# Logits of two heads issued in alternation, and large tiles placed at multiples of 1024 bytes

## Chip, cores and metric

The kernel runs on one core of one Trainium2 chip. The metric is device time in microseconds (us) of one execution; the kernel before is given as the median of three runs.

## What is computed

One layer of a decoder trunk on 256 tokens of width 2048, all in float32. From the reference, cut to what the text below uses:

```python
proj = x @ w_in[l] + b_in[l]
q, k, v, zb, uc, gl = jnp.split(proj, offs, axis=-1)
# A: dilated window attention, 24 heads of 64 (three groups of 8)
logits = jnp.einsum('brnqhd,brnkhd->brnhqk', qb, kb)
logits = jnp.where(mask, logits * (hd ** -0.5) + bias, NEG_INF)
p = jnp.exp(logits - m); den = jnp.sum(p, axis=-1, keepdims=True)
o = jnp.einsum('brnhqk,brnkhd->brnqhd', p, vb) / den
# the three groups' outputs are weighted by their denominators and summed
yb = _spatial_gating(jax.nn.gelu(zb), ...)                # B
yc = jax.nn.gelu(_s5(uc, ...)); yc = yc * sigmoid(yc @ w_glu[l] + b_glu[l])   # C
merged = gates_a * (ya @ w_pa[l]) + gates_b * (yb @ w_pb[l]) + gates_c * (yc @ w_pc[l])
x = _layer_norm(ALPHA * x + merged @ w_o[l], ln1_g[l], ln1_b[l])
gate_f, up = jnp.split(x @ w_ffn_in[l], 2, axis=-1)
x = _layer_norm(ALPHA * x + (silu(gate_f) * up) @ w_ffn_out[l], ln2_g[l], ln2_b[l])
```

## The kernel before

All large products use TensorE's fp32r type with operands split in two: a value is hi + lo, and hi*hi + hi*lo + lo*hi is summed in PSUM. A **unit** is one 512 KB block of weights (eight 128x128 blocks, or two of 128x512). For each unit SP issues a load into a `raw` tile, ScalarE copies it to `wh` (`split_h`, L262), VectorE subtracts to get `wl` (`split_l`, L268), and TensorE runs the unit's matmuls. There are four buffers of each of the three.

Two forms of unit carry the time. In a *wide* unit the activations move and the weights stand: for each of eight k-blocks a 512-column matmul (L79, hi weights against hi and lo of `xT` or `x1T`, which lie side by side) and a 256-column one (L80, lo weights). It is used for q, k, zu, uc, the gates, the GLU and the first FFN product. In a *tall* unit the weights move and 128 columns of the activations stand: three matmuls of 512 columns (L165, L166, L167; 384 columns for zv) per k-block and half of the tokens. It is used for v (`xT` stands), zv (`xT`), the output projection (`m`) and the second FFN product (`h0` for the first 12 of 44 k-blocks, and tiles `h1`... of the pool `s6` for the other 32).

The main loop over units calls `step_tasks(True)` once per unit, after the unit's matmuls are issued: it advances the generator `attention()` by one step, to its next `yield`. All engines take their instructions in this written order, SP's loads too. `attention()` is started after v; its steps fall into the 12 zu units and the 16 zv units, and are used up there.

For a pair of heads `hp` (0 to 3) and its half `e` (rows 0-63 or 64-127 of `q` and `k`), attention does: logits of the three groups for two blocks of 128 tokens, 6 matmuls in full float32 into two PSUM banks (L691, L694; each is run as two passes); softmax on VectorE and ScalarE (L699 to L706); 8 transposes and two copies (L712, L716). Each is one step, so there are three steps to a head. `values(hp)` (L662) multiplies with v for both heads of a pair, at the start of the step that issues the next pair's first logits. `load_bias` (L643) fetches a head's table of position bias for one block by four DMAs of 64 KB; two blocks are fetched one head ahead, at the step of the logits.

Tiles of SBUF come from pools in the order of first use. In the built program the pool `const` begins at byte 16512 of each partition; each tile is rounded up to 32 bytes (`bcol` 384, `ident` 512, `eps` 8, `s5keep` 576), so the large tiles begin at byte 18016, which is 608 past a multiple of 1024. `xT`/`x1T`, `x_raw`/`z0`/`z`, `raw`, `wh`, `wl` and `h0` follow without gaps in sizes that are multiples of 1024, so all of them lie at 608 past a multiple. Then comes `s5i` (96 bytes), and the eleven `s6` tiles behind it (`q`, `k`, `v`, `m`, `yb`, `yc`, `h1`..., 6144 bytes each) lie at 704 past a multiple. A 128-column block of fp32r has 512 bytes, so a block within a tile begins at 96 past a multiple of 512 in the first set, and at 192 in `s6`.

Of the kernel before, what the change touches and what calls it, by code (L numbers as in the profile page):

```python
# [10 lines left out]
F32 = mybir.dt.float32  # L11
F32R = mybir.dt.float32r
I32 = mybir.dt.int32
AF = mybir.ActivationFunctionType
ALU = mybir.AluOpType
# [10 lines left out]
NJ = 24  # L26
# [6 lines left out]
def hybrid_layer(ctx: ExitStack, tc: tile.TileContext, d: dict, out: bass.AP):  # L33
    nc = tc.nc
    const = ctx.enter_context(tc.tile_pool(name="const", bufs=1))
    sb = ctx.enter_context(tc.tile_pool(name="sb", bufs=1))
    psp = ctx.enter_context(tc.tile_pool(name="psp", bufs=1, space=bass.MemoryType.PSUM))
    dram = ctx.enter_context(tc.tile_pool(name="dram", bufs=1, space=bass.MemoryType.DRAM))
    V, A, G, T = nc.vector, nc.scalar, nc.gpsimd, nc.tensor

    RAW_BUFS, HL_BUFS, AHEAD = 4, 4, 4

    def bank(tag="mm"):
        return psp.tile([128, 512], F32, tag=tag, bufs=4, name=f"ps_{tag}")

    def tmp(n=512):

        if n <= 256:
            t = sb.tile([128, 256], F32, tag="t1", bufs=6, name="tmp1")
        else:  # L50
            t = sb.tile([128, 512], F32, tag="t2", bufs=6, name="tmp2")
        return t[:, :n]

    def s6(shape, dt, name):
        return sb.tile(shape, dt, tag="s6", bufs=11, name=name)

    def copy_split(hi, lo, src, scale=1.0):
        A.activation(hi, src, AF.Copy, scale=scale)  # L58
        if scale == 1.0:
            V.tensor_tensor(lo, src, hi.bitcast(F32), op=ALU.subtract)  # L60
        else:
            V.scalar_tensor_tensor(lo, src, scale, hi.bitcast(F32), op0=ALU.mult, op1=ALU.subtract)
# [177 lines left out]
    with tc.manual_schedule():  # L240
# [60 lines left out]
        s5 = {}  # L301
        bcol = const.tile([128, 96], F32, name="bcol")
        ident = const.tile([128, 128], F32, name="ident")


        def actx(k):
# [14 lines left out]
        big = {}  # L321
# [24 lines left out]
        def post_v(g):  # L346
            def post(ps):
                bv = big["row"]
                for t in range(2):
                    if g == 0:  # L350
                        big["v", t] = s6([128, 1536], F32, f"v{t}")
                    V.tensor_tensor(big["v", t][:, g * 512:(g + 1) * 512], ps[t], bv, op=ALU.add)
                if g == 2:
                    marks["att"] = spawn(attention(), first=True)
            return post
# [22 lines left out]

        def s5_setup():
            P = s5["P"]  # L380
            PI = sb.tile([128, NJ], I32, tag="s5i", bufs=1, name="s5i")
            keep = const.tile([128, 3, NJ, 2], F32, name="s5keep")
            bm = s6([128, 2, NJ, 32], F32, "bm")
            bb = s6([128, 2, NJ, 32], F32, "bb")
# [6 lines left out]
            def new():  # L391
                return P[:, free.pop(), :]

            pt = new()

            def ts(o, a, s1, s2, op0, op1=None):
                if op1 is None:
                    G.tensor_scalar(o, a, s1, None, op0=op0)
                else:
                    G.tensor_scalar(o, a, s1, s2, op0=op0, op1=op1)  # L400

            def tt(o, a, b, op):
                G.tensor_tensor(o, a, b, op=op)
# [7 lines left out]
            def exp(x):  # L411
# [7 lines left out]
                for c in (1.0 / 120, 1.0 / 24, 1.0 / 6, 0.5, 1.0, 1.0):  # L419
                    tt(p, p, r, ALU.mult)  # L420
                    ts(p, p, c, None, ALU.add)
                ts(PI, k, 126.0, 8388608.0, ALU.add, ALU.mult)
                tt(p, p, PI.bitcast(F32), ALU.mult)
                ts(p, p, 2.0, None, ALU.mult)
# [3 lines left out]
            th, k, r, q, x = new(), new(), new(), new(), new()  # L428
# [10 lines left out]
            n2, t, cr, ci = new(), new(), new(), new()  # L439
# [6 lines left out]
            s, c = new(), new()  # L446
# [43 lines left out]
            for c3 in range(3):  # L490
                ps = bank("sd")
                for c2 in range(2):
                    for ri in range(2):
                        c = c3 * 2 + c2
# [148 lines left out]
        def load_bias(h, t):  # L643
            bt = tmp()
            a = big["tab"][h]
            for rr in range(2):
                rq = 2 * t + rr
                for half, blk in ((0, 3 - rq), (1, 7 + 2 * (1 - rr))):
                    src = bass.AP(tensor=a.tensor, offset=a.offset + blk * 127 + 63,
                                  ap=[[L_TAB - 1, 64], [127, 4], [1, 64]])  # L650
                    nc.sync.dma_start(bt[rr * 64:(rr + 1) * 64, half * 256:half * 256 + 256]
                                      .rearrange("p (a b) -> p a b", a=4), src)
            return bt

        def attention():
            order = [(hp, e) for hp in range(4) for e in range(2)]
            big["ya"] = [s6([128, 2, 512], F32R, f"ya{i}") for i in range(2)]
            nxt = [load_bias(0, t) for t in range(2)]
            yield
            pT = [[big["z0"][:, 12 + 2 * t:14 + 2 * t, :].rearrange("p a b -> p (a b)") for t in range(2)], None]  # L660

            def values(hp):  # L662
                ya = bank("sd")
                for t in range(2):
                    for c in range(4):
                        g = max(0, c - 1)
                        vt = c if c < 2 else t
                        for e in range(2):
                            vc = (8 * g + 2 * hp + e) * 64
                            T.matmul(ya[64 * e:64 * e + 64, t * 128:(t + 1) * 128], lhsT=big["v", vt][:, vc:vc + 64],  # L670
                                     rhs=pT[e][t][:, c * 128:(c + 1) * 128], start=c == 0, stop=c == 3,
                                     tile_position=(0, 64 * e))
                y = big["ya"][hp // 2][:, hp % 2, :]
                copy_split(y[:, 0:256], y[:, 256:512], ya[:, 0:256])

            for n, (hp, e) in enumerate(order):
                if n and e == 0:
                    values(hp - 1)
                pr = slice(64 * e, 64 * e + 64)
                p = nxt  # L680
                if n + 1 < 8:
                    hp1, e1 = order[n + 1]
                    nxt = [load_bias(2 * hp1 + e1, t) for t in range(2)]
                lg = [bank("sd"), bank("sd")]
                for t in range(2):
                    for g in range(3):
                        f = 4 * g + hp
                        qa = big["q", f // 6][pr, f % 6, t * 128:(t + 1) * 128]
                        ka = big["k", f // 6][pr, f % 6, :]
                        if g == 0:  # L690
                            T.matmul(lg[t][:, 0:256], lhsT=qa, rhs=ka, start=True, stop=True)  # L691
                        else:
                            o = lg[t][:, 256:512].rearrange("p (a g i) -> p a g i", a=2, g=2)[:, :, g - 1, :]
                            T.matmul(o, lhsT=qa, rhs=ka[:, t * 128:(t + 1) * 128], start=True, stop=True)  # L694
                yield
                pn = [tmp(256), tmp(256)]
                sm = [sb.tile([128, 4], F32, tag="sm", bufs=4, name="sm") for _ in range(2)]
                for t in range(2):
                    V.tensor_tensor_reduce(p[t], lg[t], p[t], -1.0, 3.0e38, ALU.add, ALU.min, sm[t][:, 0:1])  # L699
                    A.activation(p[t], p[t], AF.Exp, bias=sm[t][:, 0:1], scale=-1.0, accum_out=sm[t][:, 1:2])  # L700
                for t in range(2):
                    V.reciprocal(sm[t][:, 2:3], sm[t][:, 1:2])
                    V.tensor_scalar(pn[t].rearrange("p (g a i) -> p a g i", a=2, g=2),
                                    p[t][:, 256:512].rearrange("p (a g i) -> p a g i", a=2, g=2),
                                    sm[t][:, 2:3], None, op0=ALU.mult)
                    V.tensor_scalar(p[t][:, 0:256], p[t][:, 0:256], sm[t][:, 2:3], None, op0=ALU.mult)  # L706
                yield
                pt = [bank("sd"), bank("sd")]
                for t in range(2):
                    for c in range(4):  # L710
                        src = (p[t] if c < 2 else pn[t])[:, (c % 2) * 128:(c % 2 + 1) * 128]
                        T.transpose(pt[t][:, c * 128:(c + 1) * 128], src, ident)  # L712
                if e == 1:
                    pT[1] = [tmp(), tmp()]
                for t in range(2):
                    A.activation(pT[e][t], pt[t], AF.Copy)  # L716
                yield
            values(3)


        def gmlp():
# [485 lines left out]
        while top_up():  # L1207
            pass
        marks["s5"] = spawn(s5_setup())
        for n, u in enumerate(units):  # L1210
            pos["n"] = n
# [138 lines left out]
```

## Time and profile before

| | before |
|---|---|
| median of 3 runs | 1602.92 us (1602.57 to 1603.49) |
| profiled execution, its own time | 1604.32 us |
| its span, first to last instruction | 1602.6 us |
| mean granted TensorE clock | 0.995 |
| TensorE busy | 99% |
| VectorE, ScalarE, GpSimd busy | 58%, 48%, 35% |
| DMA (mean busy share of 16 engines) | 0.6, 192 GB/s |

A matmul's busy time overlaps with the next one's, so rates are read here from starts: the time from the first start of a line to its last, divided by the number of steps between.

### The profile page before, as it was taken

What the parts mean: (1) busy time and instruction counts of PE and PEld (TensorE: products, weight loads), DVE (VectorE), ACT (ScalarE), POOL (GpSimd) and SP (SyncE); (2) the same over time, 40 slices, a digit from 0 to 9 for tenths busy, and PEclk for the clock granted to TensorE, in tenths of its full rate; (3) what the DMA queues carried; (4) which work ended last, traced back from release to release, by engine and by line L of the source; (5) the groups of instructions that cost most, each with busy time, mean ns of one, the idle gap of its engine ahead of it and who ended that gap; (6) DMA issues with size and microseconds to landing.
All of it is one profiled execution on the core that took longest, in us unless ns stands there. A gap on an engine that the chain in (4) does not pass through costs nothing.

```text
span 1602.6 us, 24113 instructions
## 1 busy us (share of the span) xinstructions
PE 1580.8 (99%) x9094; PEld 1366.3 (85%) x9094; DVE 931.0 (58%) x1232; ACT 763.8 (48%) x1040; POOL 559.9 (35%) x1147
## 2 busy tenths in 40 slices
PE   8999999999999999999999999999999999999996
PEld 7888888898999998889789888888888888888885
DVE  5444555556855565469667556565555555445455
ACT  5444434456544444475444545554444544333342
POOL 7569999933999999203011000000000000000002
PEclk9999999999999999999999999999999999999998
DMA  8575557655656555557863565555555556666663
GB/s 275 176 251 186 187 203 207 155 148 188 211 188 198 194 184 194 178 164 209 286 222 118 190 193 184 184 184 184 186 185 192 183 193 237 204 187 192 186 188 101
DMA packets 106492, 307.50 MB, mean 192 GB/s; under 512 B 27567, under 2 KB 28079, under 8 KB 106120
## 3 DMA queue, kind: packets, MB, share of 16 engines
q1 hardware_dynamic: 106280, 305.82, 59.7%
q8 instruction: 71, 1.16, 0.3%
q14 instruction: 45, 0.37, 0.1%
q0 software_dynamic: 96, 0.15, 0.0%
HBM read 303.78 MB, written 5.53 MB: 193 GB/s over the span
## 4 chain that ended last, share of the span: by engine, by line
PE 94%; DVE 3%; DMA 1%; ACT 1%; issue 0%; POOL 0%; SPq 0%; POOLq 0%; ACTq 0%
PE ps_mm L79 40%; PE ps_mm L80 20%; PE ps_mm L165 9%; PE ps_mm L166 9%; PE ps_mm L167 9%; DVE wl L268 1%; PE ps_mm L857 1%; PE ps_mm L858 1%; PE ps_mm L856 1%; PE ps_sd L522 1%; PE ps_sd L691 1%; PE ps_mm L108 0%; PE ps_mm L111 0%; PE ps_sd L670 0%; DMA ln<-in_ln_g_dram 0%
## 5 line engine op out<-in xcount | busy, mean ns | idle before, releaser
L268 DVE TENSOR_TENSOR wl<-raw,wh 128x1024 fp32r<-128x1024 f32 (+1 forms) x544 | 654.2, 1227 | 167.1 <-ACT wh L262 166.6
L262 ACT ACTIVATE wh<-raw 128x1024 fp32r<-128x1024 f32 (+1 forms) x544 | 556.7, 1024 | 369.1 <-PE ps_mm L167 171.6
L79 PE MATMUL ps_mm<-xT,wh 128*128 128x512 f32 x1344 | 480.6, 400 | 6.6 <-ACT wh L58 5.9
L79 PE MATMUL ps_mm<-x1T,wh 128*128 128x512 f32 x1344 | 474.9, 399 | 0.0
L80 PE MATMUL ps_mm<-xT,wl 128*128 128x256 f32 x1344 | 378.9, 282 | 0.5 <-DVE wl L268 0.5
L80 PE MATMUL ps_mm<-x1T,wl 128*128 128x256 f32 x1344 | 377.5, 281 | 0.0
L79 PEld LDWEIGHTS ps_mm<-xT,wh 128*128 128x128 f32 x1344 | 254.3, 189 | 67.1 <-ACT wh L58 5.9
L79 PEld LDWEIGHTS ps_mm<-x1T,wh 128*128 128x128 f32 x1344 | 252.6, 188 | 63.0
L937 POOL TENSOR_TENSOR z<-z,ln2w 128x512 f32<-128x512 f32 (+1 forms) x4 | 5.2, 1302 | 732.5 <-ACT z L936 732.5
L80 PEld LDWEIGHTS ps_mm<-xT,wl 128*128 128x128 f32 x1344 | 256.1, 191 | 1.5 <-DVE wl L268 0.8
L80 PEld LDWEIGHTS ps_mm<-x1T,wl 128*128 128x128 f32 x1344 | 253.9, 189 | 0.0
L546 POOL TENSOR_TENSOR X<-X,t 128x48 f32<-128x48 f32 x255 | 129.1, 506 | 48.6 <-ACT X L526 48.6
L544 POOL TENSOR_TENSOR t<-s5keep,X 128x48 f32<-128x48 f32 x254 | 126.6, 498 | 44.5 <-ACT X L526 24.7
L547 POOL TENSOR_TENSOR X<-X,t 128x48 f32<-128x48 f32 x255 | 129.9, 509 | 20.0
L166 PE MATMUL ps_mm<-wl,h 128*128 128x512 f32 x340 | 134.1, 394 | 0.0
L165 PE MATMUL ps_mm<-wh,h 128*128 128x512 f32 x340 | 134.1, 394 | 0.0
L167 PE MATMUL ps_mm<-wh,h 128*128 128x512 f32 x340 | 134.1, 394 | 0.0
L1037 DVE TENSOR_TENSOR tmp<-ps_mm,tmp 128x256 f32<-128x256 f32 x88 | 37.3, 424 | 152.9 <-ACT tmp L1036 152.9
L545 POOL TENSOR_TENSOR t<-s5keep,X 128x48 f32<-128x48 f32 x254 | 108.5, 427 | 0.0
L315 ACT ACTIVATE tmp<-ps_mm,bcol 128x256 f32<-128x256 f32 x90 | 42.7, 474 | 137.6 <-PE ps_mm L80 137.4
L1036 ACT ACTIVATE tmp<-ps_mm 128x256 f32<-128x256 f32 x88 | 33.8, 384 | 151.6 <-PE ps_mm L80 151.6
L165 PEld LDWEIGHTS ps_mm<-wh,h 128*128 128x128 f32 x340 | 64.0, 188 | 15.0
(214 smaller groups left out, 1775.6 us busy)
## 6 DMA issues: line engine op xcount, KB each, us to landing
raw<-in_w_f_dram SPq DMA_DIRECT2D x264, 512.0 KB, 4.3
raw<-in_w_b_dram SPq DMA_DIRECT2D x164, 512.0 KB, 4.6
raw<-in_w_o_dram SPq DMA_DIRECT2D x32, 512.0 KB, 5.0
raw<-in_w_v_dram SPq DMA_DIRECT2D x24, 512.0 KB, 4.0
raw<-in_w_p_dram SPq DMA_DIRECT2D x32, 384.0 KB, 3.4
raw<-in_w_zv_dram SPq DMA_DIRECT2D x16, 384.0 KB, 3.6
tmp<-tab SPq DMA_DIRECT2D x64, 64.0 KB, 3.2
raw<-in_w_p_dram SPq DMA_DIRECT2D x16, 256.0 KB, 2.9
```

What stands on the lines that cost most here:

```text
L79: T.matmul(ps, lhsT=h[:, j * 128:(j + 1) * 128], rhs=a, start=k == 0, stop=last, skip_group_check=True)
L80: T.matmul(ps[:, 0:256], lhsT=l[:, j * 128:(j + 1) * 128], rhs=a[:, 0:256], start=False, stop=last, skip_group_check=True)
L165: T.matmul(ps[:, :n], lhsT=ah, rhs=hs, start=k == 0, stop=False)
L166: T.matmul(ps[:, :n], lhsT=ah, rhs=ls, start=False, stop=False)
L167: T.matmul(ps[:, :n], lhsT=al, rhs=hs, start=False, stop=k == total - 1)
L262: A.activation(h[:, :m], raws[n][:, :m], AF.Copy)
L268: V.tensor_tensor(l[:, :m], raws.pop(n)[:, :m], h[:, :m].bitcast(F32), op=ALU.subtract)
L315: A.activation(t, ps[:, 256:512], AF.Identity, bias=bcol[:, col:col + 1], scale=scale)
L544: G.tensor_tensor(t1, keep[:, 0], prev, op=ALU.mult)
L545: G.tensor_tensor(t2, keep[:, 1], prev[:, :, ::-1], op=ALU.mult)
L546: G.tensor_tensor(cur, cur, t1, op=ALU.add)
L547: G.tensor_tensor(cur, cur, t2, op=ALU.add)
```

## The change

The eight passes of attention's loop (one per head) become four (one per pair of heads). Within a pass: one step with the 12 logits matmuls of both heads, head 0 and head 1 in turn for each block and group, into four PSUM banks; one softmax step per head; one step of transposes and copies per head, which also issues `load_bias` for the same head of the next pair; one step with `values(hp)`. The number of steps in all is 25 before the last one as before. Four bias tiles are fetched at the first step, where there were two.

Apart from that, `s5i` moves from the pool behind `h0` to `const`, and a tile of 80 floats is put behind it that nothing uses. The `const` pool becomes 96 + 320 bytes longer, so the large tiles begin at byte 18432 = 18 x 1024, and `s6`, with `s5i` gone from in front of it, at 141312 = 138 x 1024. Each tile of both sets, and so each block's offset in 512 bytes, is then 0.

```diff
+    PAD = 80
...
+        s5["i"] = const.tile([128, NJ], I32, name="s5i")
+        const.tile([128, PAD], F32, name="pad")
...
-            PI = sb.tile([128, NJ], I32, tag="s5i", bufs=1, name="s5i")
+            PI = s5["i"]
...
-            nxt = [load_bias(0, t) for t in range(2)]
-            yield
...
-            for n, (hp, e) in enumerate(order):
-                if n and e == 0:
-                    values(hp - 1)
...
-                    nxt = [load_bias(2 * hp1 + e1, t) for t in range(2)]
-                lg = [bank("sd"), bank("sd")]
...
+            p = [[load_bias(e, t) for t in range(2)] for e in range(2)]
+            yield
+            for hp in range(4):
+                lg = [[bank("sd"), bank("sd")] for _ in range(2)]
                 for t in range(2):
                     for g in range(3):
                         f = 4 * g + hp
...
+                        for e in range(2):
+                            pr = slice(64 * e, 64 * e + 64)
+                            qa = big["q", f // 6][pr, f % 6, t * 128:(t + 1) * 128]
+                            ka = big["k", f // 6][pr, f % 6, :]
+                            if g == 0:
+                                T.matmul(lg[e][t][:, 0:256], lhsT=qa, rhs=ka, start=True, stop=True)
+                            else:
+                                o = lg[e][t][:, 256:512].rearrange("p (a g i) -> p a g i", a=2, g=2)[:, :, g - 1, :]
+                                T.matmul(o, lhsT=qa, rhs=ka[:, t * 128:(t + 1) * 128], start=True, stop=True)
+                pn, sm = [None] * 2, [None] * 2
+                for e in range(2):
+                    yield
+                    pn[e] = [tmp(256), tmp(256)]
+                    sm[e] = [soft(p[e][t], lg[e][t]) for t in range(2)]
+                    for t in range(2):
+                        scale(p[e][t], sm[e][t], pn[e][t])
+                for e in range(2):
+                    yield
+                    pt = [bank("sd"), bank("sd")]
...
+                            T.transpose(pt[t][:, c * 128:(c + 1) * 128], src, ident)
...
+                        A.activation(pT[e][t], pt[t], AF.Copy)
+                    if hp < 3:
+                        p[e] = [load_bias(2 * hp + 2 + e, t) for t in range(2)]
+                yield
+                values(hp)
+                yield
```

`soft` and `scale` hold the same VectorE and ScalarE instructions as L699 to L706.

TensorE, at the first logits, before: a step with one head's six matmuls between two wide units.

```order
L80 MATMUL ps_mm<-xT,wl 128x256
L691 MATMUL ps_sd<-k_1794,q_583 128x256
L694 MATMUL ps_sd<-k_1794,q_583 128x2x64
L694 MATMUL ps_sd<-k_2083,q_1505 128x2x64
L691 MATMUL ps_sd<-k_1794,q_583 128x256
L694 MATMUL ps_sd<-k_1794,q_583 128x2x64
L694 MATMUL ps_sd<-k_2083,q_1505 128x2x64
L79 MATMUL ps_mm<-xT,wh 128x512
```

The same place in the changed program (its L80, L81, L702 and L705 are the lines L79, L80, L691 and L694 of before).

```order
L81 MATMUL ps_mm<-xT,wl 128x256
L702 MATMUL ps_sd<-k_1795,q_584 128x256 x2
L705 MATMUL ps_sd<-k_1795,q_584 128x2x64 x2
L705 MATMUL ps_sd<-k_2084,q_1506 128x2x64 x2
L702 MATMUL ps_sd<-k_1795,q_584 128x256 x2
L705 MATMUL ps_sd<-k_1795,q_584 128x2x64 x2
L705 MATMUL ps_sd<-k_2084,q_1506 128x2x64 x2
L80 MATMUL ps_mm<-xT,wh 128x512
```

Each matmul now has its twin of the other head right behind it (x2), on the other 64 rows and into another bank; the second head's step, three units later, is gone.

SP's queue at the start of attention, before (a `tmp` tile is one block's bias, `raw` a unit's weights).

```order
L251 DMA raw<-in_w_b_dram 128x1024 x7
L651 DMA tmp_2805<-tab_680 64x4x64 x4
L651 DMA tmp_2810<-tab_680 64x4x64 x4
L251 DMA raw<-in_w_b_dram 128x1024
L651 DMA tmp_2837<-tab_680 64x4x64 x4
L651 DMA tmp_2842<-tab_680 64x4x64 x4
L251 DMA raw<-in_w_b_dram 128x1024 x3
L651 DMA tmp_2955<-tab_680 64x4x64 x4
L651 DMA tmp_2960<-tab_680 64x4x64 x4
```

And in the changed program.

```order
L252 DMA raw<-in_w_b_dram 128x1024 x7
L654 DMA tmp_2806<-tab_681 64x4x64 x4
L654 DMA tmp_2811<-tab_681 64x4x64 x4
L654 DMA tmp_2816<-tab_681 64x4x64 x4
L654 DMA tmp_2821<-tab_681 64x4x64 x4
L252 DMA raw<-in_w_b_dram 128x1024 x4
L654 DMA tmp_2978<-tab_681 64x4x64 x4
L654 DMA tmp_2983<-tab_681 64x4x64 x4
L252 DMA raw<-in_w_b_dram 128x1024
L654 DMA tmp_3024<-tab_681 64x4x64 x4
L654 DMA tmp_3029<-tab_681 64x4x64 x4
```

Sixteen bias loads now stand ahead of the next weights where eight stood, and later ones come in two consecutive units with one weight load between.

## Rows read from the trace of the kernel before

**Rows 1.** The page's first and fourth part: busy time by engine, last chain by engine.

```profile
PE 1580.8 (99%) x9094; PEld 1366.3 (85%) x9094; DVE 931.0 (58%) x1232; ACT 763.8 (48%) x1040; POOL 559.9 (35%) x1147
...
PE 94%; DVE 3%; DMA 1%; ACT 1%; issue 0%; POOL 0%; SPq 0%; POOLq 0%; ACTq 0%
```

**Rows 2.** The timeline of TensorE at the first logits step: start, duration (both us).

```profile
264.32 0.28 PE L80 MATMUL ps_mm<-xT,wl 128*128 128x256 f32 x1
264.44 0.40 PE L79 MATMUL ps_mm<-xT,wh 128*128 128x512 f32 x1
264.67 0.28 PE L80 MATMUL ps_mm<-xT,wl 128*128 128x256 f32 x1
264.88 0.70 PE L691 MATMUL ps_sd<-k,q 64*128 64x256 f32 x2
265.42 0.60 PE L694 MATMUL ps_sd<-k,q 64*128 64x128 f32 x4
265.86 0.59 PE L691 MATMUL ps_sd<-k,q 64*128 64x256 f32 x2
266.29 0.60 PE L694 MATMUL ps_sd<-k,q 64*128 64x128 f32 x4
266.83 0.50 PE L79 MATMUL ps_mm<-xT,wh 128*128 128x512 f32 x1
```

**Rows 3.** The same view at a step of the state-space branch, which alternates row groups.

```profile
71.40 0.28 PE L80 MATMUL ps_mm<-xT,wl 128*128 128x256 f32 x1
71.61 1.16 PE L522 MATMUL ps_sd<-uT,bbT 32*128 32x128 f32 x16
72.70 0.50 PE L79 MATMUL ps_mm<-xT,wh 128*128 128x512 f32 x1
```

**Rows 4.** Line L165 in v, then in w_ffn_out on `h0`: count, durations (ns), first and last start.

```profile
L165 PE MATMUL ps_mm<-wh,xT x74: 389/389/389, 204.7 to 254.4; 128*128 128x512 f32 x74
...
L165 PE MATMUL ps_mm<-wh,h x17: 389/389/395, 1343.6 to 1354.5; 128*128 128x512 f32 x17
```

**Rows 5.** Line L165 in w_o on `m`, then in w_ffn_out on `s6` tiles.

```profile
L165 PE MATMUL ps_mm<-wh,m x67: 392/397/400, 773.0 to 819.4; 128*128 128x512 f32 x67
...
L165 PE MATMUL ps_mm<-wh,h x49: 389/397/400, 1357.9 to 1391.6; 128*128 128x512 f32 x49
```

**Rows 6.** Line L79 in three stretches of wide units: k, late gates, first FFN product.

```profile
L79 PE MATMUL ps_mm<-xT,wh x227: 395/398/403, 99.8 to 179.7; 128*128 128x512 f32 x114
...
L79 PE MATMUL ps_mm<-xT,wh x117: 391/391/391, 624.8 to 665.0; 128*128 128x512 f32 x117
...
L79 PE MATMUL ps_mm<-x1T,wh x1133: 395/398/403, 899.8 to 1299.8; 128*128 128x512 f32 x189
```

**Rows 7.** Line L856 (merging products, `yc` moves, three 256-column matmuls to a step).

```profile
L856 PE MATMUL ps_mm<-yc,wh x68: 278/280/283, 723.8 to 747.9; 128*128 128x256 f32 x68
```

**Rows 8.** The timeline of VectorE at the second head's softmax, first and last, and behind it.

```profile
277.51 0.69 DVE L699 CUSTOM_DVE_ANT_0 tmp<-ps_sd,tmp 128x512 f32<-128x512 f32 x1
...
280.55 0.42 DVE L706 TENSOR_SCALAR tmp<-tmp,sm 128x256 f32<-128x256 f32 x1
...
282.31 2.52 DVE L268 TENSOR_TENSOR wl<-raw,wh 128x1024 fp32r<-128x1024 f32 x2
```

**Rows 9.** The timeline of TensorE in a zv unit (tall, 384 columns).

```profile
348.25 0.33 PE L166 MATMUL ps_mm<-wl,xT 128*128 128x384 f32 x1
...
348.95 0.34 PE L167 MATMUL ps_mm<-wh,xT 128*128 128x384 f32 x1
```

**Rows 10.** The timeline of SP's queue at the start of attention, then ScalarE's.

```profile
261.59 5.26 SPq L651 DMA_DIRECT2D tmp<-tab  x8
266.96 0.54 SPq L251 DMA_DIRECT2D raw<-in_w_b_dram  x1
267.54 5.19 SPq L651 DMA_DIRECT2D tmp<-tab  x8
...
274.55 1.07 ACT L262 ACTIVATE wh<-raw 128x1024 fp32r<-128x1024 f32 x1
277.36 1.06 ACT L262 ACTIVATE wh<-raw 128x1024 fp32r<-128x1024 f32 x1 [1.74 <-DMA raw<-in_w_b_dram]
```

**Rows 11.** The page's sixth part: one weight load, median us to landing.

```profile
raw<-in_w_b_dram SPq DMA_DIRECT2D x164, 512.0 KB, 4.6
```

More of the change, by code (lines that the diff above doesn't have):

```diff
@@ L655, in attention @@
         def attention():
-            order = [(hp, e) for hp in range(4) for e in range(2)]
             big["ya"] = [s6([128, 2, 512], F32R, f"ya{i}") for i in range(2)]
-            nxt = [load_bias(0, t) for t in range(2)]
-            yield
             pT = [[big["z0"][:, 12 + 2 * t:14 + 2 * t, :].rearrange("p a b -> p (a b)") for t in range(2)], None]
@@ L674, in values, with soft, scale @@
                 copy_split(y[:, 0:256], y[:, 256:512], ya[:, 0:256])
-            for n, (hp, e) in enumerate(order):
-                if n and e == 0:
-                    values(hp - 1)
[L679 to L682, printed above, removed]
-                    nxt = [load_bias(2 * hp1 + e1, t) for t in range(2)]
-                lg = [bank("sd"), bank("sd")]
+            def soft(p, lg):
+                sm = sb.tile([128, 4], F32, tag="sm", bufs=4, name="sm")
+                V.tensor_tensor_reduce(p, lg, p, -1.0, 3.0e38, ALU.add, ALU.min, sm[:, 0:1])
+                A.activation(p, p, AF.Exp, bias=sm[:, 0:1], scale=-1.0, accum_out=sm[:, 1:2])
+                return sm
+            def scale(p, sm, pn):
+                V.reciprocal(sm[:, 2:3], sm[:, 1:2])
+                V.tensor_scalar(pn.rearrange("p (g a i) -> p a g i", a=2, g=2),
+                                p[:, 256:512].rearrange("p (a g i) -> p a g i", a=2, g=2),
+                                sm[:, 2:3], None, op0=ALU.mult)
+                V.tensor_scalar(p[:, 0:256], p[:, 0:256], sm[:, 2:3], None, op0=ALU.mult)
+            p = [[load_bias(e, t) for t in range(2)] for e in range(2)]
+            yield
+            for hp in range(4):
+                lg = [[bank("sd"), bank("sd")] for _ in range(2)]
                 for t in range(2):
@@ L687, in attention @@
                         f = 4 * g + hp
[L688 to L694, printed above, removed]
@@ L695, in attention @@
-                yield
[L696 to L706, printed above, removed]
@@ L707, in attention @@
-                yield
[L708 to L717, printed above, removed]
@@ L718, in attention @@
-            values(3)
+                        for e in range(2):
[7 more added lines that the diff above has]
+                                T.matmul(o, lhsT=qa, rhs=ka[:, t * 128:(t + 1) * 128], start=True, stop=True)
@@ new lines, in attention @@
+                pn, sm = [None] * 2, [None] * 2
[8 more added lines that the diff above has]
+                    pt = [bank("sd"), bank("sd")]
+                    for t in range(2):
+                        for c in range(4):
+                            src = (p[e][t] if c < 2 else pn[e][t])[:, (c % 2) * 128:(c % 2 + 1) * 128]
+                            T.transpose(pt[t][:, c * 128:(c + 1) * 128], src, ident)
+                    if e == 1:
+                        pT[1] = [tmp(), tmp()]
+                    for t in range(2):
+                        A.activation(pT[e][t], pt[t], AF.Copy)
+                    if hp < 3:
+                        p[e] = [load_bias(2 * hp + 2 + e, t) for t in range(2)]
```

## The prediction

> **What bounds the kernel.** I read the page first: TensorE is busy for 99% of the span and makes 94% of the chain that ended last, while no other compute engine passes 58% [rows 1]. So time is won by a shorter stream on TensorE, or lost where that stream is made to wait. Busy time doesn't say how dense the stream is, since matmuls overlap; I therefore took starts. The timeline of TensorE around a step of attention shows what a logits step costs in the stream [rows 2], and the starts of one line over a stretch show the spacing of the large matmuls [rows 4 to 7].
>
> Two things are to be seen there. First, a logits step: from the last L80 ahead of it to the first L79 behind it 266.83 - 264.67 = 2.16 us pass. A wide pair takes (179.7 - 99.8)/226 = 353.5 ns at that time [rows 6]; without the step, the L79 would have followed its L80 by 0.12 us (264.44 - 264.32 in the pair ahead [rows 2]). So a step costs 2.04 us, although it uses only 64 of the 128 rows. Second, equal matmuls don't have equal spacing. A tall 512-column matmul takes (254.4 - 204.7)/73/3 = 227 ns in v and (1354.5 - 1343.6)/16/3 = 227 ns on `h0` [rows 4], but (819.4 - 773.0)/66/3 = 234.3 ns on `m` and (1391.6 - 1357.9)/48/3 = 234.0 ns on the `s6` tiles of h [rows 5]. In rows 4 the moving weights and the standing block both lie 96 bytes past a multiple of 512; in rows 5 the moving operand is at 96 and the standing one at 192. The wide pairs have both at 96, and yet two speeds: 353.5 and (1299.8 - 899.8)/1132 = 353.4 ns in k and in the first FFN product, (665.0 - 624.8)/116 = 346.6 ns in the late gates [rows 6]. The same tiles are used at both speeds, so no address decides that one; it changes only at interruptions of the stream.
>
> **Logits in pairs.** Eight steps of 2.04 us become four. What is one of these worth? The only rows where two row groups alternate are those of the state-space branch: 16 passes of 128 columns take 72.70 - 71.40 = 1.30 us from L80 to L79 [rows 3]. In the logits the two L691 of a block make 0.54 us (264.88 to 265.42) and four passes of 128 columns 0.44 us (265.42 to 265.86), so 0.11 us each, one behind the other [rows 2]. Sixteen of them would take 1.76 us; in rows 3 they took about 0.9, the 1.30 less 0.21 ahead of the first and 0.2 behind the last. So passes on different row groups ran two at a time. Taken over to halves of 64 rows, a step for both heads has the length of one head's step, and 4 x 2.04 = **8.2 us** leave the stream. The other bound is that nothing overlaps: then only the gaps at the borders of a step (0.21 us from L80 to the first pass, and the same from the last of four L694, at 266.29 + 3 x 0.11, to L79) are saved four times, some 0.3 us each less the usual 0.12, 1.2 us in all. I take 8.2, the row being the same kind of instruction with only the size of the group changed.
>
> **What the new order could hold up.** Values, transposes and copies stay as many. Two softmaxes now come in consecutive units. One keeps VectorE for 280.97 - 277.51 = 3.5 us, and a `wl` takes 1.26 (2.52 for two) [rows 8]. Softmax, `wl`, softmax make 8.2 us behind the logits. The second head's transposes are issued four units after them: in zv a unit is 12 x 0.175 = 2.1 us ((348.95 - 348.25)/4 each [rows 9]), so at least 8.4 us and the first head's transposes later, and in zu 11.3. The `wl` in this queue belongs to a unit three further on, so it has 6.3 us or more and needs 4.8. That is covered, with some tenths of a us to spare in zv; if the cover is gone, the loss is bounded by one softmax's excess over a unit, 1.4 us, for each pair, 5 us in all. The four banks for logits: the last to come free is that of `values`, one unit earlier, and its two readers take less than a unit.
>
> SP is moved around too. Eight bias loads take 5.26 us of its queue; sixteen will take 10.5, so that the weights issued at 266.96 go out at about 272.1 [rows 10] and land 4.6 us later [rows 11], at 276.7, where ScalarE wanted them at 274.55. ScalarE splits three units ahead, 8.5 us of wide units, so TensorE doesn't see these 2.1 us. The following weights were issued behind the second eight bias loads before, at 272.7, and are no later now. In later pairs two bursts fall on two consecutive units, 10.5 us of SP for 4.2 to 5.6 us of TensorE, against four `raw` tiles of lead: no more than a us or two per pair where the lead is short. I set 0 and keep up to 3 us in the range, with the 5 above not added, since both would have to come in the same few units.
>
> **Placement.** Everything goes to 0 past a multiple of 512, so the standing block and the moving operand agree in all tall units. If agreement is what separates rows 4 from rows 5, w_o gains 4 x 16 x 2 x 3 = 384 matmuls x (234.3 - 227.0) = 2.8 us, and w_ffn_out, on 32 of its 44 k-blocks, 4 x 32 x 2 x 3 = 768 x (234.0 - 227.0) = 5.4 us: **8.2 us**. v, zv and `h0`, 227 ns and its like now, get nothing. The merging products have 192 against 96 today and take (747.9 - 723.8)/67/3 = 119.9 ns for 256 columns [rows 7], 13.2 above 256 columns at 2.4 GHz, which is what 227 is above 512 columns (13.7): nothing to gain, and a sign that an unequal offset costs only in some patterns. For the wide pairs the offsets agree before and after; their two speeds should go on to depend on how a stretch is entered, and I set 0. The bounds: all pairs at 346.6 would give back 1344 x 6.8 = 9.1 us in the first FFN product and about 576 pairs (uc, q, k, zu) x 6.9 = 4.0 us, together 13.1; the 768 pairs of the gates at 353.4 would cost 5.2.
>
> The Trainium skill ("SBUF — State Buffer", the note on SBUF cachelines) says that SBUF is read at full bandwidth as long as consecutive accesses stay in lines of 16 bytes. All offsets here, 608 and 704, are multiples of 16, so by that rule the placement would change nothing, and the sum would be the pairing's 8.2 alone; the 7 ns between rows 4 and 5 speak for a dependence that the rule doesn't have.
>
> **Sum.** The profiled execution took 1604.3 us, 1.4 above the median. 1604.3 - 8.2 - 8.2 = 1587.9 for it, and 1602.9 - 16.4 = **1586.5 us** for the median.
>
> **Rivals.**
> - *Placement does nothing.* What differs between rows 4 and 5 is then something else, as which unit stands ahead. Against it: within w_ffn_out the same code changes its spacing exactly where the k-blocks leave `h0`. 1602.9 - 8.2 = 1594.7 us.
> - *Wide pairs fall into the faster speed as well.* For it: that speed exists and is kept over 280 us of the gates. Against it: their relative offsets don't change. 1586.5 - 13.1 = 1573.4, or 1577.4 with the first FFN product alone.
> - *The two halves don't overlap.* 1602.9 - 1.2 - 8.2 = 1593.5 us. Rows 3 speak against it.
> - *Multiples of 1024 collide.* With every tile on one phase, standing and moving reads of the wide pairs could meet at L79 and L80 as they do in rows 5. At 7.2 ns for one matmul of each of 2688 pairs, that is 19.4 us: 1605.9; for both, 1625. It turns the sign from 16.4/2688 = 6.1 ns per pair on. Against it: in rows 4 both operands already have one phase in 512 bytes, at the best spacing.
> - *TensorE waits in attention* for softmax or weights, and placement does nothing: 1594.7 + 5 + 3 = 1602.7, no change.
>
> **How the numbers follow.** The forecast, 0.45; faster wide pairs, 0.25; placement without effect, 0.15; no overlap, 0.05; collision, 0.07; waits, 0.03. About 0.2%, 3.2 us, is what a measurement here can tell from no change. The first four are faster by more than that, 0.90; same 0.03; slower 0.07. The range from 1571 to 1596 holds the first four with their bounds of a few us, nine tenths less what lies at their edges.
>
> **What would show it.** Right: each logits step, both heads, still about 2.2 us from L81 to L80 of the new numbering, and four of them; L165's matmuls (L166 in the changed file) at 227 ns on `m` and on all of h; wide pairs at 353 and 347 ns in the stretches where they are now. Wrong: logits steps near 4 us; 234 ns kept in w_o; wide pairs at another spacing than these two, or 347 in the first FFN product; waits of TensorE for `wl`, `tmp` or weights between 262 and 362 us.

## The result and the profile after

| | before | after |
|---|---|---|
| median | 1602.93 us (1602.57 to 1603.49, 4 runs) | 1589.94 us (1588.63 to 1590.49, 4 runs) |
| profiled execution, its span | 1604.32, 1602.6 us | 1590.49, 1588.7 us |
| mean granted TensorE clock | 0.995 | 0.995 |

The ratio is 0.9919 [0.9908, 0.9931]: 13.0 us faster, where 16.4 were forecast; the time lies in the range, 3.4 us above the forecast.

The page of after, its busy times and its last chain, answers to [rows 1]: the bound is the same.

```profile
PE 1566.2 (99%) x9094; PEld 1359.8 (86%) x9094; DVE 931.2 (59%) x1232; ACT 762.9 (48%) x1040; POOL 557.8 (35%) x1147
...
PE 94%; DVE 3%; DMA 1%; ACT 1%; issue 1%; POOL 0%; SPq 0%; POOLq 0%; ACTq 0%
```

With a stream this full, time is told by where the stages start. Each number of this table is the time from the first matmul of a stage to the first of the next (us, profiled runs; w_ffn_out to the start of its last step). The columns on the right are experiments of the next section. Left out are the merging of c (34.6 us, 33.6 in `off32`) and the first four tiles of the first FFN product (about 25 us), which before and after have alike, and what lies ahead of the first matmul and behind the last.

| stage | before | after | pair_only | place_only | not_alternated | off32 | rephase_one |
|---|---|---|---|---|---|---|---|
| uc, q, k | 187.93 | 187.94 | 186.43 | 186.41 | 185.02 | 187.00 | 188.89 |
| v | 65.31 | 65.31 | 65.31 | 65.31 | 65.31 | 67.19 | 65.31 |
| zu | 46.87 | 43.54 | 43.59 | 46.86 | 45.02 | 43.54 | 43.53 |
| zv | 56.61 | 51.90 | 51.90 | 56.63 | 53.37 | 52.00 | 51.89 |
| gates, merging a, b | 329.51 | 332.36 | 329.52 | 332.28 | 332.28 | 331.07 | 331.40 |
| GLU | 23.71 | 24.03 | 23.71 | 24.03 | 24.03 | 23.78 | 24.03 |
| w_o | 93.16 | 90.48 | 91.61 | 90.04 | 89.61 | 92.48 | 90.58 |
| first FFN product | 474.88 | 474.88 | 474.88 | 474.88 | 474.88 | 474.88 | 466.10 |
| w_ffn_out | 244.58 | 238.71 | 244.59 | 238.71 | 238.71 | 243.83 | 238.72 |

From before to after, zu and zv give 3.33 + 4.71 = 8.04 us and w_o and w_ffn_out 2.68 + 5.87 = 8.55; gates and GLU take back 2.85 + 0.32 = 3.17. These make 13.4 of the span's 13.9.

The timeline of TensorE in after at the first logits step (start and duration in us) answers to [rows 2].

```profile
264.30 0.28 PE L81 MATMUL ps_mm<-xT,wl 128*128 128x256 f32 x1
264.50 0.70 PE L702 MATMUL ps_sd<-k,q 64*128 64x256 f32 x4
265.04 0.61 PE L705 MATMUL ps_sd<-k,q 64*128 64x128 f32 x8
265.48 0.60 PE L702 MATMUL ps_sd<-k,q 64*128 64x256 f32 x4
265.92 0.61 PE L705 MATMUL ps_sd<-k,q 64*128 64x128 f32 x8
266.46 0.50 PE L80 MATMUL ps_mm<-xT,wh 128*128 128x512 f32 x1
```

266.46 - 264.30 = 2.16 us, for twice the matmuls: the second head's passes ran wholly beside the first's. The four steps take 2.16, 2.17, 2.22 and 2.22 us, where the eight of before took 2.15 to 2.22.

The next rows are lines of after over a stretch (count, durations in ns, first and last start): L166 on `m` and on the `s6` tiles of h, which answer to [rows 5]; L80 in k, in the late gates and in the first FFN product, which answer to [rows 6]; and a merging product with `yc`, which answers to [rows 7].

```profile
L166 PE MATMUL ps_mm<-wh,m x47: 388/389/390, 774.7 to 806.0; 128*128 128x512 f32 x47
...
L166 PE MATMUL ps_mm<-wh,h x50: 388/390/390, 1345.2 to 1378.6; 128*128 128x512 f32 x50
...
L80 PE MATMUL ps_mm<-xT,wh x227: 394/398/404, 99.8 to 179.7; 128*128 128x512 f32 x114
...
L80 PE MATMUL ps_mm<-xT,wh x114: 394/399/404, 614.8 to 654.7; 128*128 128x512 f32 x114
...
L80 PE MATMUL ps_mm<-x1T,wh x1133: 394/399/404, 889.8 to 1289.8; 128*128 128x512 f32 x189
...
L866 PE MATMUL ps_mm<-yc,wh x96: 282/284/284, 710.6 to 744.8; 128*128 128x256 f32 x96
```

The tall matmuls now follow each other at (806.0 - 774.7)/46/3 = 226.8 and (1378.6 - 1345.2)/49/3 = 227.2 ns in both places, where they took 234. The wide pairs keep 353.5 in k and 353.4 in the first FFN product, but the late gates went from 346.6 to (654.7 - 614.8)/113 = 353.1 ns: a third of the 3.17 us is lost there, most of the rest in the early gates. In these rows and in [rows 6] the durations show it as well, 391 ns for the 512-column matmul of the faster speed and about 398 for that of the slower.

The waits in after from 255 to 365 us (waiting line, releaser: us, times, longest) show whether the new order held up TensorE.

```profile
ACT wh L263 <- DMA raw<-in_w_zv_dram: 10.2, 4, 3.9
...
DVE tmp L679 <- DMA tmp<-tab: 1.3, 2, 1.0
...
PEld ps_sd L702 <- issue: 1.0, 4, 0.3
```

ScalarE waited for weights, up to 3.9 us at a time, and VectorE for a bias. None of TensorE's own waits in this view is longer than 0.3 us; the largest group is the entry into the four logits steps.

### The profile page after: what moved, and what is told of

It reads as the page before. It is cut to its first block, busy times and chain, and to the rows that moved or that the text cites. A ratio compares the mean times of both kernels' runs of the same rounds, so it can differ in the third digit from the quotient of the medians.

```text
span 1588.7 us, 24112 instructions
## 1 busy us (share of the span) xinstructions
PE 1566.2 (99%) x9094; PEld 1359.8 (86%) x9094; DVE 931.2 (59%) x1232; ACT 762.9 (48%) x1040; POOL 557.8 (35%) x1147
## 4 chain that ended last, share of the span: by engine, by line
PE 94%; DVE 3%; DMA 1%; ACT 1%; issue 1%; POOL 0%; SPq 0%; POOLq 0%; ACTq 0%
PE ps_mm L80 40%; PE ps_mm L81 20%; PE ps_mm L166 9%; PE ps_mm L167 9%; PE ps_mm L168 9%; DVE wl L269 2%; PE ps_mm L868 1%; PE ps_mm L867 1%; PE ps_mm L866 1%; PE ps_sd L525 1%; PE ps_mm L109 0%; PE ps_mm L112 0%; PE ps_sd L670 0%; DMA raw<-in_w_o_dram 0%; PE ps_sd L719 0%
## 5 line engine op out<-in xcount | busy, mean ns | idle before, releaser
L263 ACT ACTIVATE wh<-raw 128x1024 fp32r<-128x1024 f32 (+1 forms) x544 | 556.7, 1024 | 371.0 <-PE ps_mm L168 169.1
L80 PE MATMUL ps_mm<-xT,wh 128*128 128x512 f32 x1344 | 482.6, 402 | 7.5 <-ACT wh L59 5.5
L80 PE MATMUL ps_mm<-x1T,wh 128*128 128x512 f32 x1344 | 474.9, 399 | 0.0
L81 PE MATMUL ps_mm<-xT,wl 128*128 128x256 f32 x1344 | 379.8, 283 | 0.4 <-DVE wl L269 0.4
L81 PE MATMUL ps_mm<-x1T,wl 128*128 128x256 f32 x1344 | 378.0, 281 | 0.0
L80 PEld LDWEIGHTS ps_mm<-xT,wh 128*128 128x128 f32 x1344 | 254.7, 190 | 69.5 <-ACT wh L59 5.5
L80 PEld LDWEIGHTS ps_mm<-x1T,wh 128*128 128x128 f32 x1344 | 252.9, 188 | 62.7
L81 PEld LDWEIGHTS ps_mm<-xT,wl 128*128 128x128 f32 x1344 | 256.8, 191 | 1.2 <-DVE wl L269 0.7
L81 PEld LDWEIGHTS ps_mm<-x1T,wl 128*128 128x128 f32 x1344 | 254.5, 189 | 0.0
L547 POOL TENSOR_TENSOR t<-s5keep,X 128x48 f32<-128x48 f32 x254 | 132.3, 521 | 44.2 <-ACT X L529 24.4
L550 POOL TENSOR_TENSOR X<-X,t 128x48 f32<-128x48 f32 x255 | 129.0, 506 | 20.0
L166 PE MATMUL ps_mm<-wh,h 128*128 128x512 f32 x340 | 132.4, 390 | 0.0
L168 PE MATMUL ps_mm<-wh,h 128*128 128x512 f32 x340 | 132.4, 390 | 0.0
L549 POOL TENSOR_TENSOR X<-X,t 128x48 f32<-128x48 f32 x255 | 115.0, 451 | 40.5 <-ACT X L529 40.5
L548 POOL TENSOR_TENSOR t<-s5keep,X 128x48 f32<-128x48 f32 x254 | 116.4, 458 | 0.0
L1046 ACT ACTIVATE tmp<-ps_mm 128x256 f32<-128x256 f32 x88 | 33.6, 382 | 152.0 <-PE ps_mm L81 152.0
L166 PEld LDWEIGHTS ps_mm<-wh,h 128*128 128x128 f32 x340 | 63.9, 188 | 13.3
```

The costliest lines, as they stand in the source:

```text
L80: T.matmul(ps, lhsT=h[:, j * 128:(j + 1) * 128], rhs=a, start=k == 0, stop=last, skip_group_check=True)
L81: T.matmul(ps[:, 0:256], lhsT=l[:, j * 128:(j + 1) * 128], rhs=a[:, 0:256], start=False, stop=last, skip_group_check=True)
L166: T.matmul(ps[:, :n], lhsT=ah, rhs=hs, start=k == 0, stop=False)
L168: T.matmul(ps[:, :n], lhsT=al, rhs=hs, start=False, stop=k == total - 1)
L263: A.activation(h[:, :m], raws[n][:, :m], AF.Copy)
L547: G.tensor_tensor(t1, keep[:, 0], prev, op=ALU.mult)
```

## The experiments

Ratios are against the kernel before, timed beside each experiment (its medians: 1602.45 to 1602.77 us). Diffs are against the kernel after unless another is named.

**The two parts alone.** `pair_only` has the new attention and the old placement:

```diff
-    PAD = 80
...
-        s5["i"] = const.tile([128, NJ], I32, name="s5i")
-        const.tile([128, PAD], F32, name="pad")
...
-            PI = s5["i"]
+            PI = sb.tile([128, NJ], I32, tag="s5i", bufs=1, name="s5i")
```

> The new order of attention alone, tiles where they were before. Theory (the pairing saves 8.0 us in zu and zv, the placement the rest): zu and zv together 8.0 us shorter than before, w_o and the second half of w_ffn_out at 234 ns as before; 1594.8 us if the gates' wide pairs go on at 347 ns, 1598 if they go at 352 as in the changed kernel. Rival (the two parts need each other, since the pairing is only free with aligned q and k tiles): less than 6 us saved in zu and zv.

Measured: 1593.18 us, 0.9945 [0.993, 0.9959]. `place_only` is the reverse, the kernel before with the new placement:

```diff
+    PAD = 80
...
+        s5["i"] = const.tile([128, NJ], I32, name="s5i")
+        const.tile([128, PAD], F32, name="pad")
...
-            PI = sb.tile([128, NJ], I32, tag="s5i", bufs=1, name="s5i")
+            PI = s5["i"]
```

> The placement alone, attention as before. Theory: w_o 2.7 and w_ffn_out 5.9 us shorter; zu and zv as before. If the gates' loss of 3.2 us in the changed kernel comes from the placement, the gates are 3 us longer here too and the time is 1597.4; if it comes from the new order of attention (another entry into the stage), the gates keep 329.5 us and the time is 1594.3.

Measured: 1597.1 us (1596.36 to 1598.99, 7 runs), 0.9967 [0.9956, 0.9979]. The same two lines as above, L165 of h and L79 of the late gates, in `pair_only`:

```profile
L165 PE MATMUL ps_mm<-wh,h x49: 389/397/400, 1348.2 to 1382.0; 128*128 128x512 f32 x49
...
L79 PE MATMUL ps_mm<-xT,wh x116: 391/391/391, 614.9 to 654.8; 128*128 128x512 f32 x116
```

and in `place_only` (L166 and L80 there):

```profile
L80 PE MATMUL ps_mm<-xT,wh x115: 395/398/403, 619.7 to 660.0; 128*128 128x512 f32 x115
...
L166 PE MATMUL ps_mm<-wh,h x45: 389/389/389, 1351.8 to 1381.8; 128*128 128x512 f32 x45
```

Pairing alone leaves 234.7 ns on h and 347.0 in the late gates; placement alone brings 227.3 and 353.5. In the table the parts add up: zu and zv by pairing; w_o, w_ffn_out, gates (+2.77) and GLU by placement. So the loss in the gates belongs to the placement, and isn't a delayed cost of attention.

The medians of the parts, -9.6 and -5.7, don't add up to -13.0. The table shows where executions differ from one to the next. The first stage takes 185.0 to 188.9 us, in before and after 1.5 us more than in the two parts, and 1.1 to 1.4 us of this are there already 240 matmuls into the stage (47.06 and 47.17 us after its start, against 45.92 and 45.73). TensorE's waits for its first tiles, which vary from run to run, fall in this part. Some 20 us into w_o TensorE waits for split weights, 1.1 us in before and after, 0.8 in `place_only` and not at all in `pair_only`. So stages, not medians, carry the argument below 2 us.

The clock plays hardly any part in this, though it did fall. Behind the small matmuls of the bias tables TensorE was granted its lower level (1.2 of 2.4 GHz) in the profiled runs of before and after, for 3.4 us. The columns are window, its us, PE, PEld, VectorE, ScalarE and GpSimd busy (count), granted clock, DMA share, GB/s. Before:

```profile
62.10:65.50 3.40, 3.40 (x13) 2.92 (x12) 1.98 (x3) 0.00 (x0) 3.32 (x2) 0.51 0.21 36
```

`pair_only`, and its wait in this window:

```profile
62.10:65.50 3.40, 2.42 (x18) 2.00 (x17) 2.21 (x3) 0.73 (x2) 2.50 (x1) 1.00 0.38 119
...
PE ps_sd L495 <- POOL bb L486: 1.0, 1, 1.0
```

At the full clock TensorE waited there for GpSimd instead. Between the 240th and the 320th matmul before and after lost 0.1 to 0.4 us against the parts.

**Is it the multiple of 1024, or that both operands agree?** `all_at_96` puts every large tile 96 bytes past a multiple of 1024:

```diff
-    PAD = 80
+    PAD = 104
```

> The changed kernel with the pad 24 floats longer: all large tiles lie at 96 past a multiple of 1024, none at a multiple. Theory (what counts is that moving and standing operand have the same offset): w_o and w_ffn_out at 227 ns as in the changed kernel, 1590 us within 3 us, whatever the gates' pairs do. Rival (multiples of 1024, or of 64, are what counts): 234 ns again, 1598 us.

Measured: 1589.89 us, 0.9922 [0.9907, 0.9937], with L166 on h in this kernel at (1378.7 - 1344.7)/50/3 = 226.7 ns:

```profile
L166 PE MATMUL ps_mm<-wh,h x51: 389/389/389, 1344.7 to 1378.7; 128*128 128x512 f32 x51
```

So the multiple of 1024 isn't what counts; for the tall units it is enough that both operands have the same offset.

This kernel also says what slows the gates. It has the attention of `pair_only`, and `xT` and the weights lie at 96 past a multiple of 512 in both kernels; of the two sets only `s6` differs, at 192 there and at 96 here. Its gates take 332.28 us, against 329.52. L80 in its late gates runs at (654.7 - 614.8)/113 = 353.1 ns, where `pair_only` had 347.0:

```profile
L80 PE MATMUL ps_mm<-xT,wh x114: 395/398/403, 614.8 to 654.7; 128*128 128x512 f32 x114
```

Of `s6` the large matmuls of this stage read `ya` and `yb`, the moving operands of the merging products. In after (and alike in `place_only` and `all_at_96`) of the stretches of 16 pairs that nothing else interrupted, those behind merging products with `ya` ran at the slower speed, and of those behind `yb` every second one did, as these two in a row show:

```profile
L80 PE MATMUL ps_mm<-xT,wh x16: 390/392/398, 493.1 to 498.3; 128*128 128x512 f32 x16
...
L80 PE MATMUL ps_mm<-xT,wh x16: 395/398/404, 500.8 to 506.1; 128*128 128x512 f32 x16
```

In before and `pair_only` all such stretches ran at 347 ns.

How much disagreement is enough? `off32` moves `xT` 32 bytes down and `s6` 32 up, the weights and `h0` staying at 0; `off64` does so by 64 (`PAD = 64`, gaps of 16 floats).

```diff
-    PAD = 80
+    PAD = 72
...
         xT = sb.tile([128, KD, 512], F32R, tag="t32", bufs=1, name="xT")
+        sb.tile([128, 8], F32, tag="gap1", bufs=1, name="gap1")
...
+        sb.tile([128, 8], F32, tag="gap2", bufs=1, name="gap2")
```

> The changed kernel with xT and x1T 32 bytes lower and the s6 tiles 32 bytes higher than a multiple of 1024, wh and wl still at a multiple. Theory (any unequal offset costs): w_o and w_ffn_out's second part over 230 ns, v and zv (where xT stands) too. Rival (only offsets like the 96 of before cost, and 32 bytes are within what the reads tolerate): 227 ns in all four. The wide pairs: 353 in the first FFN product if only the entry counts, another spacing if the offset does.

> The same with 64 bytes instead of 32. Theory (any unequal offset costs): over 230 ns in w_o and w_ffn_out. Rival (the reads go by lines of 64 bytes, and only a start within a line costs): 227 ns.

Measured, one run each: 1596.22 and 1595.18 us. The tall lines of `off32` in v, w_o and on h, and a merging product:

```profile
L166 PE MATMUL ps_mm<-wh,xT x71: 393/396/397, 204.7 to 253.7; 128*128 128x512 f32 x71
...
L166 PE MATMUL ps_mm<-wh,m x57: 395/396/397, 766.2 to 805.4; 128*128 128x512 f32 x57
...
L166 PE MATMUL ps_mm<-wh,h x49: 389/395/396, 1349.9 to 1383.4; 128*128 128x512 f32 x49
...
L868 PE MATMUL ps_mm<-yc,wh x96: 277/279/281, 710.5 to 743.7; 128*128 128x256 f32 x96
```

v went up to 233.3 ns, w_o is at 233.3 again and h at 232.6: 32 bytes cost nearly as much as the 96 of before (w_ffn_out keeps 0.75 of its 5.87 us). But zv, where the same `xT` stands and 384 columns move, kept its time (52.00 us, after 51.90). The merging products, in which the 256 columns of `yc` move, gained instead: (743.7 - 710.5)/95/3 = 116.5 ns, after 120.0. The same tall lines of `off64`:

```profile
L166 PE MATMUL ps_mm<-wh,xT x72: 388/388/388, 205.1 to 253.9; 128*128 128x512 f32 x72
...
L166 PE MATMUL ps_mm<-wh,m x57: 393/393/398, 766.3 to 805.5; 128*128 128x512 f32 x57
...
L166 PE MATMUL ps_mm<-wh,h x49: 389/393/398, 1350.2 to 1383.7; 128*128 128x512 f32 x49
```

w_o and h are at 233.3 and 232.6 ns as in `off32`, but v, with `xT` 64 bytes below, is only at (253.9 - 205.1)/71/3 = 229.1. Every unequal offset tried cost the 512-column tall matmuls something, and the amount isn't a matter of the distance alone.

**What do the halves owe to the alternation?** `not_alternated` issues all six matmuls of head 0, then those of head 1:

```diff
-                    for g in range(3):
-                        f = 4 * g + hp
-                        for e in range(2):
+                    for e in range(2):
+                        for g in range(3):
+                            f = 4 * g + hp
```

(the order within a block of 128 tokens.)

> The changed kernel, but within a block of 128 tokens the three logits matmuls of head 0 are issued ahead of the three of head 1. Theory (passes overlap where neighbours in the queue are on different row groups): only the pairs at the turn from one head to the other overlap, a logits step takes 3.5 to 3.9 us, and zu and zv are 5.5 to 7 us longer than in the changed kernel: 1596 us. Rival (the queue finds the other head's passes wherever they stand): steps of 2.2 us, no difference.

Measured: 1592.3 us (1589.92 to 1592.6), 0.9937 [0.992, 0.9953]; zu and zv together 2.95 us longer than after. The timeline of TensorE in this kernel at the first logits step:

```profile
261.71 0.28 PE L81 MATMUL ps_mm<-xT,wl 128*128 128x256 f32 x1
261.92 0.70 PE L702 MATMUL ps_sd<-k,q 64*128 64x256 f32 x2
262.45 0.27 PE L705 MATMUL ps_sd<-k,q 64*128 64x128 f32 x1
262.46 0.48 PE L702 MATMUL ps_sd<-k,q 64*128 64x256 f32 x1
262.56 0.38 PE L705 MATMUL ps_sd<-k,q 64*128 64x128 f32 x2
...
264.61 0.50 PE L80 MATMUL ps_mm<-xT,wh 128*128 128x512 f32 x1
```

The step takes 264.61 - 261.71 = 2.90 us, between the 2.16 of full overlap and the 4.2 of two single steps. The fourth and fifth row show why: L702 of head 1 starts at 262.46 beside L705 of head 0, though it is written behind head 0's passes. This lies between the two expectations: passes overlap that aren't neighbours in the written order, but only in part where the halves don't alternate.

**What sets the speed of a wide pair?** `phase_probe` puts one extra small matmul ahead of every twelfth unit of the first FFN product, of 8, 16, ... 112 columns, into a bank that nothing reads:

```diff
+            w = n - marks["f1"] - 8
+            if w >= 0 and w % 12 == 10 and w < 168:
+                c = 8 * (w // 12) + 8
+                T.matmul(bank("sd")[:, :c], lhsT=hl[n][0][:, 0:128], rhs=big["x1T"][:, 0, 0:c], start=True, stop=True)
```

> The changed kernel with 14 extra matmuls in the first FFN product, one ahead of every twelfth wide unit, of 8, 16, ... 112 columns, into a bank that nothing reads. Theory (the speed of the wide pairs is set by how the stream is entered): behind some of them the pairs run at 347 ns until the next one, behind others at 353. Rival (something fixed in this stage sets 353): all stay at 353 ns, and the time grows by 14 x 0.05 to 0.1 us, 1 us.

Measured, one run: 1584.0 us, although work was added. L80 in the stretches behind the extra matmuls of 8, 64 and 72 columns:

```profile
L80 PE MATMUL ps_mm<-x1T,wh x87: 391/391/391, 889.9 to 919.7; 128*128 128x512 f32 x87
...
L80 PE MATMUL ps_mm<-x1T,wh x92: 395/398/403, 1121.6 to 1153.8; 128*128 128x512 f32 x92
...
L80 PE MATMUL ps_mm<-x1T,wh x94: 392/394/395, 1155.7 to 1187.9; 128*128 128x512 f32 x94
```

346.5, 353.8 and 346.2 ns. Behind 8 to 56 columns all stretches run at the faster speed; behind 64, 80, 96 and 112 at the slower, behind 72, 88 and 104 at the faster. From 64 columns on, each extra matmul thus turned the speed over, and whether the columns or the speed before it decide isn't told apart by this run. The tiles, offsets and matmuls of the pairs are the same throughout, so what is put ahead of a stretch decides, and a stretch keeps its speed until something else is put into the stream.

Two attempts to make use of it missed. `rephase` puts an 8-column matmul ahead of one unit in each of five stretches, `rephase3` ahead of three consecutive units in each of three:

```diff
+            if n in (26, marks["a"] + 20, marks["glu"] - 26, marks["glu"] - 3, marks["f1"] + 8):
+                a = big["x1T"] if n > marks["f1"] else xT
+                T.matmul(bank("sd")[:, 0:8], lhsT=hl[n][0][:, 0:128], rhs=a[:, 0, 0:8], start=True, stop=True)
```

```diff
+            if any(0 <= n - m < 3 for m in (26, marks["glu"] - 25, marks["f1"] + 9)):
```

> The changed kernel with five extra matmuls of 8 columns, each at the start of a stretch whose wide pairs ran at 353 ns (k, first gates, late gates, GLU, first FFN product), into a bank that nothing reads. Theory (the speed is set by the phase at which a stretch is entered, and 8 columns lead to the faster one): 1344 pairs of the first FFN product gain 6.7 ns each, 9.0 us; k 1.8, the late gates 1.1, first gates and GLU up to 2; less 5 x 0.09: 1576 to 1579 us. Rival (the gain of the probe came from being entered again and again, and the faster speed decays): the first FFN product stays over 473 us long, 1585 us or more.

> The changed kernel with nine extra matmuls of 8 columns: one ahead of each of three consecutive units at the start of k's quiet stretch, of the late gates and of the first FFN product. The slow pairs go round in three (361, 349, 350 ns), and a unit is eight pairs, so the three meet the three places in that round. Theory (the speed is a matter of phase; the probe's first one, met at the place after 350, led to the faster speed and the faster speed survives further ones): 347 ns for nearly all of the first FFN product, 8.6 us less; k 1.5 and the late gates 0.7 less: 1579 us. Rival (what the probe found hung on the longer matmuls behind the first): 353 ns stays, 1590.5 us.

Measured: 1589.85 us, 0.9921 [0.9906, 0.9936], and 1590.05 us, 0.9922 [0.9909, 0.9936], both like after. In `rephase` the first FFN product stayed slow. In `rephase3` L80 shows one unit and then the rest of that product:

```profile
L80 PE MATMUL ps_mm<-x1T,wh x13: 391/392/473, 862.9 to 867.2; 128*128 128x512 f32 x13
...
L80 PE MATMUL ps_mm<-x1T,wh x1275: 395/398/403, 869.7 to 1319.9; 128*128 128x512 f32 x183
```

The first extra matmul made the pairs fast, the third made them slow again. So `rephase_one` keeps only the first, in the late gates and in the first FFN product:

```diff
+            if n in (marks["glu"] - 25, marks["f1"] + 9):
+                a = big["x1T"] if n > marks["f1"] else xT
+                T.matmul(bank("sd")[:, 0:8], lhsT=hl[n][0][:, 0:128], rhs=a[:, 0, 0:8], start=True, stop=True)
```

> The changed kernel with two extra matmuls of 8 columns: ahead of the second unit of the wide pairs in the first FFN product, and ahead of the second unit of the late gates. In the run with three at each place the first led to the faster speed, the second kept it and the third lost it again. Theory (the speed is a matter of phase alone, and each stretch keeps what its entry gave it): 346.7 ns for 1335 pairs of the first FFN product, 8.9 us less, and for 150 pairs of the late gates, 1.0 us less, minus 2 x 0.09: 1580 us. Rival (the faster speed is lost again within a stretch so long): over 1585 us.

Measured: **1579.79 us** (1579.24 to 1581.6, 4 runs), 0.9858 [0.9842, 0.9875], faster than both kernels. L80 in the first FFN product of this kernel:

```profile
L80 PE MATMUL ps_mm<-x1T,wh x1328: 391/391/391, 864.7 to 1324.7; 128*128 128x512 f32 x190
```

346.6 ns to the end: 474.88 - 466.10 = 8.8 us for one matmul of 8 columns, and 1.0 in the gates for the other.

## Why the prediction was right, and where it was off

- **What bounds the kernel**: right. The stages that changed with the edits, in the table, did so by TensorE's stream.
- **Logits in pairs**, -8.2: right, -8.04 in zu and zv. A step for both heads takes 2.16 us as one did, so the overlap taken over from [rows 3] holds for halves of 64 rows. `not_alternated` shows that it comes from the halves running side by side.
- **What the new order could hold up**, 0: right for TensorE, which has no wait over 0.3 us there. ScalarE's waits for weights came to 10.2 us, up to 3.9 at a time, more than the "us or two per pair" of the text; they stayed behind its lead, as argued for SP's queue.
- **Placement of the tall units**, -8.2: right, -8.55 (w_o's share includes its varying wait, 1.1 us in both kernels), and the reason, agreement of the two offsets, stands by `place_only`, `all_at_96`, `off32` and `off64`. By the Trainium skill's rule on 16-byte lines ("SBUF — State Buffer", the note on SBUF cachelines) nothing should have moved. The measurement shows a dependence that the rule doesn't have: unequal offsets of 32, 64 and 96 bytes, multiples of 16 all, cost 5 to 7 ns per matmul in w_o and on h, and 2 to 6.5 in v.
- **Wide pairs**, 0: this is the mis-sized term. It should have been **+3.2**, inside the bound of +5.2 that the text had worked out for the gates. The prediction saw that "it changes only at interruptions of the stream", yet took the entries to stay as they were. They didn't: the gates are entered from merging products, whose operands now agree, and behind them most stretches run at 353 (`all_at_96` beside `pair_only`). At 6.8 ns a pair, 3.17 us are what some 470 pairs cost. So one of the text's own signs of being right, 347 ns in the stretches that had it, failed in the gates.
- **Faster wide pairs** (chance 0.25): not with this change; `rephase_one` shows that the speed was there to be had for the first FFN product, with 8.8 us of the bound's 9.1.
- **Collision at 1024** (0.07): refuted, in after pairs took only their two known speeds and `all_at_96` gives the same time.

The sum with this one term put right, 1602.9 - 8.2 - 8.2 + 3.2 = 1589.7 us, is within 0.3 us of the measured time; the other two terms missed by 0.2 and 0.35 us in opposite directions.

Three things stay open: why a disagreement of 32 bytes costs a tall matmul 6 ns, why 64 cost v only 2, and what the phase is measured against. That the slower gates come from `s6` is shown by `all_at_96` beside `pair_only`; that they come by the phase at which merging products hand over is argued, since `ya` and `yb` weren't moved by themselves. Nor were different offsets for wide and merging products tried beside equal ones for the tall, or extra matmuls of another size or place in the early gates and in k, where the 8 columns of the two first attempts hadn't the wanted effect.

## What to carry to other kernels

Read the spacing of equal matmuls stretch by stretch, from starts: a stream that is 99% busy can hold 2 to 3% that no busy share shows. If the spacing differs by tile, compare the offsets of the moving and standing operands; if it differs by stretch with the same tiles, look at how the stretch is entered, and price any edit that alters an entry at both speeds. Matmuls that use half of the rows belong next to their twins on the other half: 2.16 us a step here, against 2.90 one head after the other.

## What the runs showed that was not expected

- One matmul of 8 columns, in the right place, makes the 1328 pairs behind it 6.8 ns shorter each, and another some units later undoes it (`rephase_one`, `rephase3`). From 64 columns on, each extra matmul turned the speed over (`phase_probe`).
- An offset of 32 bytes between moving and standing operand costs a 512-column tall matmul 6 ns, nearly what 96 do; a 256-column merging product gains 3.5 ns by the same shift, and the 384-column ones of zv don't change.
- TensorE overlaps matmuls on different halves of the rows that stand some instructions apart: 2.90 us for a step written one head after the other.
- The granted clock fell to its lower level for 3.4 us behind the small table matmuls in two profiled runs, and not in others of nearly the same program; it cost at most 0.4 us, as the others had a wait for GpSimd in that stretch.
